# A mixture-of-experts decoder block on one Trainium2 core: six split operations of the next expert's weights move to later steps of the order

## The chip, the cores and the metric

One core of a Trainium2 chip runs the kernel. Its engines are TensorE (PE in the profile, with its weight loads as PEld), VectorE (DVE), ScalarE (ACT), GpSimd (POOL) and SyncE (SP, which here only issues DMAs). The metric is the device time of one execution in microseconds; the kernel before took 1094.59 us in the median of three runs (1091.77 to 1094.7).

## What is computed

A decoder block over 1024 tokens of width 1024 in float32: a gated mixer (a chunked gMLP beside sliding-window attention), a residual sum, then a mixture of 16 experts and a last RMSNorm. Each token goes to two of the 16 experts. The part that matters here is the experts:

```python
for e in range(N_EXPERTS):
    hid = jax.nn.silu(t @ w_gate[e]) * (t @ w_up[e])
    out = out + combine[:, e:e + 1] * (hid @ w_down[e])
```

`w_gate[e]` and `w_up[e]` are 1024 x 512, `w_down[e]` is 512 x 1024. The kernel computes an expert only on the tokens that chose it.

## The kernel before

The products have float32 accuracy, made of three products of numbers that TensorE takes at full rate: every operand is split into a **high part** (a rounded copy, made by ACT) and a **low part** (operand minus high part, made by DVE), and `mm3` (lines 198 to 201) adds high x high, high x low and low x high in PSUM.

**Stages.** After the mixer and the routing (to about 650 us) the tokens lie sorted by expert in DRAM. The loop at line 1674 runs through 16 stages, `e` = 0 to 15, an expert each; a table sets which expert comes when, by its count of tokens. A stage has a **first tile** (the first 128 tokens, or fewer, always computed, `expert_tile`, line 1352) and, only if the expert has more than 128 tokens, a **last tile**, which is computed before the rest of the first tile (`last_tile`, line 1552): a **half tile** for up to 64 more tokens (`half_tile`, line 1461; its names end in `h`), otherwise a full one (names ending in `l`). In this run stages 2, 4, 6, 8 and 10 have a half tile, stages 12 and 15 a full last tile, and stages 3, 5, 7, 9, 11, 13 and 14 none.

**An expert's weights** come as 12 granules of 128 x 1024 numbers (512 KB): granules 0 to 7 hold gate and up (two DMAs of 256 KB each), 8 to 11 down. During stage `e` the granules of the expert of stage `e + 1` are split: `granules.high(g)` is an ACT copy (line 299), `granules.low(g)` a DVE subtraction (line 305 for granules 0 to 7, line 309 for 8 to 11). There are nine raw buffers, so the load of granule `g + 9` is issued behind the low part of `g` (`load_others`, line 315). All loads are issued by SP, in the order of the granules.

**The order of a stage.** Granules 0, 1 and 2 are split at the start (beside the last tile). The table `AHEAD` (line 51) says behind which step of the first tile each further high part (`h3`) and low part (`l3`) is written, for stages 2 to 14. The steps of `expert_tile` are:

- `("k", 0..3)`: gate and up products of the first four granules, for both halves `f` of the hidden width
- `("f0", 5)`: behind granules 4 and 5 of half 0; granules 6 and 7 follow
- then `hidden(0)`: the silu of half 0 (ACT, line 1368) and **the product of activations**, silu times up (DVE, line 1369)
- `("f1", 5)`: behind granules 4 and 5 of half 1; then `hidden_T(0)`: TensorE transposes the product (line 1375), ACT and DVE split it (lines 176 and 177, tile `hT`)
- granules 6 and 7 of half 1, then `hidden(1)`, then `("f1", 7)`
- `down(0)` (line 1413), `hidden_T(1)`, `("y", 0)`, `down(1)`, `("y", 1)`, `down(2)`, `("y", 2)`, `down(3)`

At `("y", 1)` the next stage's tokens X are transposed and split ahead of the table's entries (`transpose_x`, line 1312, tile `xT`; lines 1325, 176, 177). At `("k", 2)` SP loads the tokens of the next stage's last tile into `xt_last` (`last_rows`, line 1444; lines 1453 to 1458), and only if that stage has one. A half tile begins with the transposes of `xt_last` (line 1472) and their split (tile `xT_last`).

An engine runs its instructions in its own order and waits at the head of it. TensorE's, SP's and GpSimd's are taken as written; the order of ACT and DVE comes from a scheduler that follows the written order.

Of the kernel before, what the change touches and what calls it, by code (L numbers as in the profile page):

```python
# [48 lines left out]
FIRST = 3  # L49

AHEAD = {
    ("k", 1): "h3 l3", ("k", 2): "h4 l4", ("k", 3): "h5 l5", ("f0", 5): "h6 l6",
    ("f1", 5): "h7 l7 h8", ("f1", 7): "l8 h9", ("y", 0): "l9 h10", ("y", 1): "l10 h11", ("y", 2): "l11",
}

AHEAD_0 = {("f1", 7): "h3 l3 h4 l4", ("y", 0): "h5 l5 h6 l6 h7 l7", ("y", 1): "h8 l8 h9 l9 h10 l10 h11 l11"}
# [1879 lines left out]
```

## Time and profile before

| What | Value |
|---|---|
| Median of three runs | 1094.59 us (1091.77, 1094.59, 1094.7) |
| The profiled execution's own time | 1091.46 us |
| Its span, first to last instruction | 1089.7 us |
| Mean granted TensorE clock | 0.98 of full speed |
| PE busy | 1023.1 us, 94% of the span |
| DVE busy | 724.8 us, 67% |
| ACT busy | 608.7 us, 56% |
| DMA, mean over the span | 197 GB/s |

The profiled execution is 3.13 us below the median. All times of rows are counted from the start of its span. In a row of the timeline the first number is the start, the second the duration, and what stands in brackets is how long the engine sat idle ahead of it and what ended that. Rows of one line and tile that follow each other without a gap are merged (x3).

### The profile page before, as it was taken

The numbers are of one execution on the slowest core, as the hardware profiler recorded it, in microseconds if no ns is written. First come the engines' busy times: TensorE is split into PE (matmuls) and PEld (weight loads), VectorE is DVE, ScalarE is ACT, GpSimd is POOL, SyncE is SP. The second block draws the span as 40 slices with busy tenths as digits, with TensorE's granted clock in tenths as the row PEclk, the third lists the DMA queues.
The fourth block names the chain that finished last, engine by engine and source line by source line (L and its number), as shares of the span: only waits on it lengthen the run. The fifth ranks groups of instructions, "written<-read, shape, count | busy, mean of one in ns | idle before, by whom it ended". The sixth has DMA issues, their size and how long they took to land. (4 is left out here: it accounts for less than half of the span.)

```text
span 1089.7 us, 15458 instructions
## 1 busy us (share of the span) xinstructions
PE 1023.1 (94%) x4775; PEld 821.1 (75%) x4775; DVE 724.8 (67%) x1584; ACT 608.7 (56%) x1016; POOL 107.6 (10%) x132
## 2 busy tenths in 40 slices
PE   7999899999999999999999958899999999999893
PEld 6778788788888888887888846677777777777682
DVE  6852577675368555776445788978769686848735
ACT  5543465543356464555335447676858686847743
POOL 4001000000004000000001041111111112010020
PEclk9999999999999999999999989999999999999997
DMA  8432545645137413222646546969898989979854
GB/s 248 122 106 102 173 157 166 188 140 184 44 120 273 140 54 97 83 72 68 203 152 215 196 175 223 330 241 319 281 334 258 313 293 285 306 240 309 252 218 191
DMA packets 125478, 214.47 MB, mean 197 GB/s; under 512 B 11563, under 2 KB 58731, under 8 KB 125360
## 3 DMA queue, kind: packets, MB, share of 16 engines
q1 hardware_dynamic: 112016, 176.58, 48.6%
q0 software_dynamic: 7200, 21.20, 7.0%
q10 hardware_dynamic: 6144, 15.27, 3.8%
q8 instruction: 56, 0.92, 0.3%
q14 instruction: 62, 0.51, 0.1%
HBM read 185.46 MB, written 37.63 MB: 205 GB/s over the span
## 5 line engine op out<-in xcount | busy, mean ns | idle before, releaser
L305 DVE SCALAR_TENSOR_TENSOR w_e<-raw_e,g2T,w_e 128x1024 fp32r<-128x1024 f32 x127 | 156.1, 1280 | 22.9 <-ACT w_e L299 16.6
L299 ACT ACTIVATE w_e<-raw_e,g2T 128x1024 fp32r<-128x1024 f32 x127 | 137.5, 1142 | 15.1 <-DMA raw_e<-in_expert_w_up_dram 4.5
L199 PE MATMUL ps_gu<-w_e,xT 128*128 128x512 f32 x256 | 104.2, 407 | 8.9 <-ACT w_e L299 4.1
L201 PE MATMUL ps_gu<-w_e,xT 128*128 128x512 f32 x256 | 101.8, 398 | 1.1 <-DVE xT L177 1.1
L1413 PE MATMUL ps_y<-w_e,hT 128*128 128x512 f32 x384 | 100.4, 404 | 1.1 <-DVE hT L177 0.9
L200 PE MATMUL ps_gu<-w_e,xT 128*128 128x512 f32 x256 | 101.5, 396 | 0.0
L1413 PEld LDWEIGHTS ps_y<-w_e,hT 128*128 128x128 f32 x384 | 69.9, 190 | 17.3 <-DVE hT L177 1.8
L309 DVE TENSOR_TENSOR w_e<-raw_e,w_e 128x1024 fp32r<-128x1024 f32 x63 | 75.0, 1218 | 0.8 <-ACT w_e L299 0.8
L299 ACT ACTIVATE w_e<-raw_e 128x1024 fp32r<-128x1024 f32 x63 | 65.7, 1054 | 0.4 <-DMA raw_e<-in_expert_w_down_dram 0.2
L199 PEld LDWEIGHTS ps_gu<-w_e,xT 128*128 128x128 f32 x256 | 48.7, 190 | 20.7 <-issue 9.7
L201 PEld LDWEIGHTS ps_gu<-w_e,xT 128*128 128x128 f32 x256 | 48.8, 190 | 12.9 <-DVE xT L177 1.5
L200 PEld LDWEIGHTS ps_gu<-w_e,xT 128*128 128x128 f32 x256 | 48.8, 191 | 10.1
L201 PE MATMUL ps_o<-w_wo,ms 128*128 128x512 f32 x128 | 51.3, 402 | 0.0
L200 PE MATMUL ps_o<-w_wo,ms 128*128 128x512 f32 x128 | 51.1, 400 | 0.0
L199 PE MATMUL ps_o<-w_wo,ms 128*128 128x512 f32 x128 | 51.1, 399 | 0.0
L199 PE MATMUL ps_ga<-xh,w_ga 128*128 128x512 f32 x128 | 50.8, 397 | 0.0
L200 PE MATMUL ps_ga<-xh,w_ga 128*128 128x512 f32 x128 | 50.7, 396 | 0.0
L201 PE MATMUL ps_ga<-xh,w_ga 128*128 128x512 f32 x128 | 50.6, 396 | 0.0
L200 PE MATMUL ps_gb<-xh,w_gb 128*128 128x512 f32 x128 | 50.6, 395 | 0.0
L201 PE MATMUL ps_gb<-xh,w_gb 128*128 128x512 f32 x128 | 50.6, 395 | 0.0
L199 PE MATMUL ps_gb<-xh,w_gb 128*128 128x512 f32 x128 | 50.6, 395 | 0.0
L567 PE MATMUL ps_gv<-w_gv,xh 128*128 128x512 f32 x192 | 46.9, 397 | 3.9 <-ACT xh L176 2.5
(540 smaller groups left out, 2379.8 us busy)
## 6 DMA issues: line engine op xcount, KB each, us to landing
raw_e<-in_expert_w_gate_dram SPq DMA_DIRECT2D x127, 256.0 KB
raw_e<-in_expert_w_up_dram SPq DMA_DIRECT2D x127, 256.0 KB
raw_e<-in_expert_w_down_dram SPq DMA_DIRECT2D x63, 512.0 KB
xs_d<-zero ACTq DMA_DIRECT2D x16, 516.0 KB
xt_last<-xs_d SPq DMA_DIRECT2D x32, 258.0 KB
raw_ga<-in_w_in_dram SPq DMA_DIRECT2D x16, 512.0 KB
raw_gb<-in_w_in_dram SPq DMA_DIRECT2D x16, 512.0 KB
raw_wo<-in_w_out_dram SPq DMA_DIRECT2D x16, 512.0 KB
```

The lines of the kernel that those rows point to most:

```text
L199: nc.tensor.matmul(acc, lhi, rhi, start=start, stop=False)
L200: nc.tensor.matmul(acc, lhi, rlo, start=False, stop=False)
L201: return nc.tensor.matmul(acc, llo, rhi, start=False, stop=stop)
L299: nc.scalar.activation(self.split_tiles[g][:, 0, :], self.raw[g], AF.Copy, **scale)
L305: nc.vector.scalar_tensor_tensor(w[:, 1, :], raw, g2T[:, k : k + 1], w[:, 0, :], ALU.mult, ALU.subtract)
L309: nc.vector.tensor_tensor(w[:, 1, :], raw, w[:, 0, :], ALU.subtract)
L567: nc.tensor.matmul(accs[i], xh[a][k // 4][:, k % 4, t], gs[j][:, b, k % 2, :], start=k + a + b == 0, stop=k == KT - 1 and b == 1,)
L1413: nc.tensor.matmul(ys[nh], hT[:, a, k, :], dn[k][:, b, nh * 512 : (nh + 1) * 512], start=k + i == 0, stop=k == FK - 1 and i == 2,)
```

## The change

Only the table `AHEAD` changes: six of the nine low parts that it orders move a step down, high parts stay where they are.

```diff
 AHEAD = {
-    ("k", 1): "h3 l3", ("k", 2): "h4 l4", ("k", 3): "h5 l5", ("f0", 5): "h6 l6",
-    ("f1", 5): "h7 l7 h8", ("f1", 7): "l8 h9", ("y", 0): "l9 h10", ("y", 1): "l10 h11", ("y", 2): "l11",
+    ("k", 1): "h3 l3", ("k", 2): "h4 l4", ("k", 3): "h5 l5", ("f0", 5): "h6", ("f1", 5): "l6 h7 h8",
+    ("f1", 7): "l7 h9", ("y", 0): "l8 h10", ("y", 1): "l9 l10 h11", ("y", 2): "l11",
 }
```

The fourth low part of the first tile, `l6`, goes from `("f0", 5)` behind `hidden(0)`; `l7`, `l8` and `l9` follow a step later each. So `l9`, `l10` and `l11` come behind the split of the next X, where before it was `l10` and `l11`.

Stage 5 (no last tile), DVE, before, from the fourth low part of the first tile to the split of the next X (`w_e` with `g2T` are low parts of granules 0 to 7, without it of 8 to 11; here 5300 is granule 6, 5367 is 7, 5376 is 8, 5525 is 9; the two ISA rows compute the tokens' weights `cw`):

```order
L305 SCALAR_TENSOR_TENSOR w_e_5300<-raw_e_5370,g2T,w_e_5300 128x1024
L1369 TENSOR_TENSOR hid_0_8831<-hid_0_8831,ps_gu_0_8459 128x256
L305 SCALAR_TENSOR_TENSOR w_e_5367<-raw_e_5373,g2T,w_e_5367 128x1024
L177 TENSOR_TENSOR hT_8751<-ps_hT_0_8848,hT_8751 128x256
L1369 TENSOR_TENSOR hid_1_8859<-hid_1_8859,ps_gu_1_8460 128x256
L1399 ISA parts,cw_8862<-meta_8418,own 128x4
L1399 ISA cw_8862 128x1
L309 TENSOR_TENSOR w_e_5376<-raw_e_5379,w_e_5376 128x1024
L177 TENSOR_TENSOR hT_8751<-ps_hT_1_8877,hT_8751 128x256
L309 TENSOR_TENSOR w_e_5525<-raw_e_5382,w_e_5525 128x1024
L177 TENSOR_TENSOR xT_5985<-ps_xT_0_8894,xT_5985 128x512
L177 TENSOR_TENSOR xT_5985<-ps_xT_1_8899,xT_5985 128x512
```

The same place with the change, from the first product of activations to granule 9:

```order
L1369 TENSOR_TENSOR hid_0_8828<-hid_0_8828,ps_gu_0_8459 128x256
L305 SCALAR_TENSOR_TENSOR w_e_5300<-raw_e_5370,g2T,w_e_5300 128x1024
L177 TENSOR_TENSOR hT_8751<-ps_hT_0_8845,hT_8751 128x256
L1369 TENSOR_TENSOR hid_1_8856<-hid_1_8856,ps_gu_1_8460 128x256
L1399 ISA parts,cw_8859<-meta_8415,own 128x4
L1399 ISA cw_8859 128x1
L305 SCALAR_TENSOR_TENSOR w_e_5367<-raw_e_5373,g2T,w_e_5367 128x1024
L177 TENSOR_TENSOR hT_8751<-ps_hT_1_8874,hT_8751 128x256
L309 TENSOR_TENSOR w_e_5376<-raw_e_5379,w_e_5376 128x1024
L177 TENSOR_TENSOR xT_5985<-ps_xT_0_8891,xT_5985 128x512
L177 TENSOR_TENSOR xT_5985<-ps_xT_1_8896,xT_5985 128x512
L309 TENSOR_TENSOR w_e_5525<-raw_e_5382,w_e_5525 128x1024
```

One low part fewer stands ahead of the first product, ahead of both splits of `hT` and ahead of the split of X, and one more behind that. It is so in each of stages 2 to 14.

Stage 5, ACT, with the change, from the high part of granule 6 to the split of the first `hT`; before, the order is the same:

```order
L299 ACTIVATE w_e_5300<-raw_e_5370,g2T 128x1024
L1368 ACTIVATE hid_0_8828<-ps_gu_0_8459 128x256
L299 ACTIVATE w_e_5367<-raw_e_5373,g2T 128x1024
L299 ACTIVATE w_e_5376<-raw_e_5379 128x1024
L176 ACTIVATE hT_8751<-ps_hT_0_8845 128x256
```

Nothing moves here: the split of `hT` stands behind the high parts of granules 7 and 8. The order of ACT, PE, POOL and SP is the same in the whole program.

## Rows read from the trace of the kernel before

**Rows 1.** What TensorE waited for, 690 to 1035 us: us in total, times, longest us.

```profile
PE ps_hT L1375 <- DVE hid L1369: 11.0, 11, 4.0
...
PE ps_xT_8h L1472 <- DMA xt_last<-xs_d: 0.7, 1, 0.7
...
PE ps_xT_12l L1325 <- DMA xt_last<-xs_d: 0.5, 1, 0.5
```

**Rows 2.** Stages 4, 5: PE, PEld, DVE, ACT, POOL busy; clock, DMA share, GB/s.

```profile
751.00:782.00 31.00, 30.65 (x141) 24.16 (x139) 21.90 (x35) 20.31 (x30) 6.10 (x4) 1.00 0.83 279
782.00:801.00 19.00, 17.92 (x85) 14.27 (x83) 16.86 (x21) 15.97 (x21) 2.00 (x2) 1.00 1.03 328
```

**Rows 3.** Timeline of DVE, stage 5 and the start of stage 6.

```profile
783.86 8.47 DVE L305 SCALAR_TENSOR_TENSOR w_e<-raw_e,g2T,w_e 128x1024 fp32r<-128x1024 f32 x7 [0.85 <-issue]
792.24 0.42 DVE L1369 TENSOR_TENSOR hid<-hid,ps_gu 128x256 f32<-128x256 f32 x1
...
798.65 1.29 DVE L177 TENSOR_TENSOR xT<-ps_xT,xT 128x512 fp32r<-128x512 f32 x2 [0.48 <-ACT xT L176]
799.86 2.35 DVE L309 TENSOR_TENSOR w_e<-raw_e,w_e 128x1024 fp32r<-128x1024 f32 x2
802.22 0.29 DVE L177 TENSOR_TENSOR xT_last<-ps_xT_6h,xT_last 128x128 fp32r<-128x128 f32 x1
```

**Rows 4.** Timeline of ACT, stage 5, around the first product of activations.

```profile
790.27 0.38 ACT L1368 ACTIVATE hid<-ps_gu 128x256 f32<-128x256 f32 x1 [0.26 <-PE ps_gu L201]
...
792.07 1.04 ACT L299 ACTIVATE w_e<-raw_e 128x1024 fp32r<-128x1024 f32 x1
```

**Rows 5.** Timeline of PE, stage 5: the transposes and the first product of `down(0)`.

```profile
792.71 0.44 PE L1375 MATMUL ps_hT<-ident,hid 128*128 128x128 f32 x2 [1.08 <-DVE hid L1369]
...
794.38 0.40 PE L1413 MATMUL ps_y<-w_e,hT 128*128 128x512 f32 x1
```

**Rows 6.** Timeline of PE, stage 4 (half tile): the first products of `down(0)`.

```profile
775.17 0.62 PE L1413 MATMUL ps_y<-w_e,hT 128*128 128x512 f32 x2
```

**Rows 7.** Timeline of ACT, stage 4: split of the first `hT`.

```profile
774.54 0.36 ACT L176 ACTIVATE hT<-ps_hT 128x256 fp32r<-128x256 f32 x1
```

**Rows 8.** Timeline of PE: the half tiles of stages 6 and 8.

```profile
801.16 0.71 PE L1472 MATMUL ps_xT_6h<-ident,xt_last 64*128 64x64 f32 x8
...
803.29 1.09 PE L1491 MATMUL ps_gu_6h<-w_e,xT_last 128*128 128x512 f32 x4
...
852.50 0.68 PE L1472 MATMUL ps_xT_8h<-ident,xt_last 64*128 64x64 f32 x8 [0.69 <-DMA xt_last<-xs_d]
```

**Rows 9.** DMA in 40 slices of 0.2 us, 795 to 803 us.

```profile
GB/s 430 379 430 369 420 379 420 411 401 405 419 259 103 228 167 227 195 185 216 206 246 246 277 236 256 297 348 399 348 246 236 328 318 369 379 359 399 348 348 369
```

**Rows 10.** The same, 846 to 854 us.

```profile
GB/s 389 461 451 328 420 369 421 379 431 342 428 267 186 158 217 176 92 145 185 185 258 236 185 174 164 174 236 256 338 318 389 318 266 236 348 348 318 266 420 358
```

**Rows 11.** Timeline of ACT and PE, stage 14.

```profile
1022.11 1.15 ACT L299 ACTIVATE w_e<-raw_e,g2T 128x1024 fp32r<-128x1024 f32 x1 [3.41 <-DMA raw_e<-in_expert_w_up_dram]
1023.17 0.36 ACT L1368 ACTIVATE hid<-ps_gu 128x256 f32<-128x256 f32 x1
...
1024.96 0.44 PE L1375 MATMUL ps_hT<-ident,hid 128*128 128x128 f32 x2 [3.98 <-DVE hid L1369]
```

**Rows 12.** Windows, two waits and what follows: PE busy, clock, DMA share, GB/s.

```profile
678.77:681.55 2.78, 0.01 (x1) 1.00 1.02 355
681.55:685.00 3.45, 3.44 (x15) 1.00 1.03 362
...
1025.30:1028.70 3.40, 3.40 (x10) 0.51 1.06 318
```

**Rows 13.** SP, stage 4: the first load behind the low part of granule 9.

```profile
779.71 0.33 SPq L280 DMA_DIRECT2D raw_e<-in_expert_w_gate_dram  x1
```

**Rows 14.** DMA, 773.5 to 781.6 us: what moved, and what was issued (gate halves).

```profile
DMA packets 1082, 1.98 MB, mean 244 GB/s; under 512 B 116, under 2 KB 116, under 8 KB 1082
...
raw_e<-in_expert_w_gate_dram SPq DMA_DIRECT2D x6, 256.0 KB
```

## The prediction, made blind

> **What bounds the kernel now.** I read the list of waits first, then the windows of two neighbouring stages, then the timelines of DVE, ACT and PE around the moved low parts, and last DMA and SP. TensorE is busy 94% of the span, so only its waits can go. From stage 2 to stage 14 nearly all of its waiting is one wait, the transposes of `hidden_T(0)` for the product of activations: 11.0 us in 11 waits, the longest 4.0 [rows 1]. Ten short ones share the other 7, in stages 2 to 11; stage 5's is 1.08 [rows 5]. The second thing to see is the DMA system. In stage 4, with a half tile, its share is 0.83; in stage 5, without one, 1.03 [rows 2]. So in odd stages the weights stream without a pause, and two rows for DMA `xt_last` (0.7 and 0.5 us, stages 8 and 12) show who is late behind that stream [rows 1].
>
> **Odd stages (3, 5, 7, 9, 11).** In stage 5 DVE runs seven low parts without a break, 8.47/7 = 1.21 us each, and then the product at 792.24 [rows 3]. ACT's silu is ready at 790.27 + 0.38 = 790.65 [rows 4]. Without the seventh low part the product starts at 792.24 - 1.21 = 791.03, after the silu, so the silu is no new wait. PE arrived at 792.71 - 1.08 = 791.63 [rows 5], and the product would end at 791.03 + 0.42 = 791.45. The whole wait of 1.08 goes.
>
> Not all of it arrives. The next in line, `down(0)`, needs ACT's split of `hT`, which the order puts behind the high part of granule 8. That ends at 792.07 + 1.04 = 793.11 [rows 4], the split takes 0.36 [rows 7], so `down(0)` starts at about 793.5 in place of 794.38 [rows 5]: 0.88 gained. The low part itself isn't saved: it runs behind the product, in time that DVE has.
>
> **Even stages (2, 4, 6, 8, 10).** In stage 4 the split of `hT` starts at 774.54 without idle time ahead of it and ends at 774.90 [rows 7], pinned behind the same high part, and `down(0)` starts at 775.17 [rows 6]. Whatever DVE gives, 775.17 - 774.95 = 0.22 is the gain. Together 1.1 per pair of stages, if nothing follows.
>
> **What is late next: the half tile behind an odd stage.** Two gates stand there. The first is DVE. Before, the two low parts between the split of X and `xT_last` end at 799.86 + 2.35 = 802.21 [rows 3]. Now there are three. X's split starts 1.1 earlier, at 797.55, ends at 798.84, and three low parts of 1.18 end at 802.4. The split of `xT_last` is then 0.2 later than before, and can cost a further 0.1 where the third is 1.2 long. Before, it ended at 802.51 and its products began at 803.29 [rows 3, 8], so 0.78 lay between. With PE 1.1 earlier and the split 0.2 to 0.3 later, 0.5 of the 1.1 is eaten, and some 0.55 per pair is left.
>
> The second gate is `xt_last` itself. SP issues it behind weights that fill the queues. In stage 8 PE waits 0.69 for it and starts at 852.50 [rows 8]; DMA's rate had come back over 300 GB/s at 846 + 28 x 0.2 = 851.6 [rows 10], 0.9 earlier. In stage 6 PE shows no wait, starting at 801.16 [rows 8]; the rate comes back at 795 + 26 x 0.2 = 800.2 [rows 9], 0.96 earlier. By that likeness `xt_last` came just in time in stage 6. The stream doesn't depend on the moved low parts but on the loads that earlier ones released, so PE's getting there earlier turns into this wait. I take 0.2 for each of the pairs that end ahead of stages 4, 6 and 10 (the return can be read to within two slices of 0.2 us, so the slack lies between 0 and 0.4, and I take the middle) and 0 for those ahead of 8 and 12, where the wait is there already. Sum: 0.6. The Trainium skill, "DMA: Bandwidth & Descriptors", Specifications, gives about 358 GB/s as the most that HBM feeds a core; slices here show over 400 [rows 9], so no sum of mine goes by it, but the 328 GB/s of stage 5 is close enough that a faster stream isn't to be expected.
>
> **Stages 12 and 13.** They show no wait of this kind worth a row: 0.
>
> **Stage 14.** High part 6 waits 3.41 us for its weights, the silu ends at 1023.17 + 0.36 = 1023.53, and PE starts at 1024.96 after 3.98 us [rows 11]. In between lie low part 6 (1.21 to 1.28) and the product (0.42). Without the low part PE starts at about 1024.03: 0.93 gained, with no half tile behind it. The wait becomes 3.05. Then the clock: after the 3.98 the granted clock was 0.51, the level of 1.2 GHz, and 3.40 us held 10 matmuls; after an earlier wait of 2.78 us it stayed at 1.00 (2.4 GHz), and 3.45 us held 15 [rows 12]. Ten at full rate are 2.3 us, so up to 1.15 more can come back, and at least 0. 3.05 is nearer to 2.78 than to 3.98, so I take the clock as staying; as `hT`'s split is again behind a high part, I count 0.9. The Trainium skill, "TensorE: Matmul & The Clock Gate", HAM oscillation, tells of waits for DMA behind which matmuls start at half rate; the 3.98 agrees with it, the 2.78 shows the other side, and by that rule alone stage 14 would give only 0.93.
>
> **Queues.** The low parts' moves carry the loads behind them. SP issues granule 9's first load at 779.71 in stage 4 [rows 13]; behind X's split (0.48 idle and 1.29 [rows 3]) it comes at about 781.5. From 773.5 to 781.6 six granules of 2 x 256 KB were issued and 1.98 MB moved [rows 14]. Without granule 9's own, 2.62 - 1.98 = 0.64 MB are still queued at 781.6, 1.6 us at 400 GB/s. So I cost it at nothing; the cover is that queue. The loads of 6, 7 and 8 move by one step (about 1 us) with more queued. In odd stages SP is behind in the stream anyway. POOL's queue passes none of the moved rows. The three low parts behind X's split have no reader on PE before the next stage.
>
> **Sum.** 0.6 + 0 + 0.93 + 0.9 = 2.4 us off the profiled execution's 1091.46, or 1089.0. That execution is 3.13 below the median, so on the scale of the runs I predict 1094.59 - 2.4 = **1092.2 us**. About 0.3% (3.3 us) is what a measurement of this kernel can tell from no change; the three runs shown differ by nearly that.
>
> **Rivals.**
> - *The clock falls in stage 14 all the same* (chance 0.22). For it: 3.05 is still a long wait. Then 0.6 + 0.93 = 1.5, 1093.1 us.
> - *The stream of weights isn't a gate* (0.25): `xt_last` comes with PE's pace, because the loads of the stage before, moved too, leave room for it. Then DVE's gate decides: 5 x 0.55 = 2.75, with stage 14's 0.93 to 1.83 3.7 to 4.6; about 1090.4 us. Against it: the two DMA waits that already stand in stages 8 and 12.
> - *Slower: the queue runs empty in even stages* (0.10). If the time from SP's issue to the first packet exceeds the 1.6 us of cover, DMA stands still, granules of the odd stage come that much later, and as that stage has a share of 1.03 nothing catches up: the loss comes out at `xt_last`. At 1 us in each of five pairs, 5 less stage 14's 0.93 is 4.1 more: 1098.7 us. It decides from the point where 0.64 MB is gone before granule 9's load begins. Against it: later granules were queued before too, and DVE reaches low part 11 at the same time.
> - *The change does nothing that the time shows* (0.05): DVE's order does change, but the gain is taken by the two gates and stage 14's DMA; 1094.6 us.
>
> **How the numbers follow.** The forecast has 0.38. Faster by over 0.3% needs 3.3 us: most of the second rival and a share of the forecast's spread, 0.29. Slower by over 0.3%: the third rival and a little spread, 0.09. Within: 0.62. The range reaches from the second rival's end with the runs' spread, 1089.2, to the last one's with the same, 1095.8; left out are most of the slower case and the far tails.
>
> **What would show it.** In the profile after, the wait for the product (11.0 us) should fall to about 3 us, nearly all in stage 14, with 3.05 as its longest. `down(0)` of stage 5 should start 0.88 earlier against the stage's begin, behind ACT. The wait for DMA `xt_last` should grow to stages 4, 6, 8, 10 and 12, some 0.9 each; if instead the half tile's products wait for DVE's `xT_last`, the second rival holds. In stage 14 the clock behind the wait tells forecast from first rival. A share of DMA below 1 in stage 5, or waits of ACT for weights there, would show the third. I am wrong if the even or odd stages' length changes by over 0.6 us a pair.

## The result: slower by 0.6%, and the profile after

The changed kernel took 1101.03 us in the median of 16 runs (1095.94 to 1106.3), the kernel before 1094.64 us in 16 runs beside them (1091.33 to 1097.88). The ratio is 1.0061, with a 95% interval of 1.0046 to 1.0077: **6.4 us slower**, where 2.4 us faster was forecast.

The profiled execution after took 1104.78 us (span 1103.0 us), 3.75 above its median, while that of before lay 3.18 below the median of its 16 runs. So the two profiles differ by more (13.3 us) than the kernels do. Part of that lies ahead of the changed stages: the first `hT` of stage 0 comes 1.86 us later, and stage 1 adds 2.5 us, with a granted clock of 0.50 from 684 to 688 us where before showed 1.00. What follows counts from the half tile of stage 2.

The list of waits of TensorE after the change, 698 to 1056 us (columns as in [rows 1]):

```profile
PE ps_y L1413 <- ACT hT L176: 7.9, 12, 1.9
...
PE ps_xT_12l L1325 <- DMA xt_last<-xs_d: 1.9, 1, 1.9
PE ps_xT_8h L1472 <- DMA xt_last<-xs_d: 1.6, 1, 1.6
PE ps_xT_10h L1472 <- DMA xt_last<-xs_d: 1.1, 1, 1.1
PE ps_xT_4h L1472 <- DMA xt_last<-xs_d: 0.9, 1, 0.9
```

The wait for the product of activations (11.0 us in [rows 1]) is off the head of the list. Two kinds of wait have come in its place: 7.9 us of `down(0)` for ACT's split of `hT`, and four for `xt_last` of 5.5 us together (1.2 in [rows 1]). A wait of 2.15 us for weights at the start of stage 13 only looks new: the same instruction waited 1.63 us before, put down to another releaser (before, then after):

```profile
992.52 0.47 PE L199 MATMUL ps_gu<-w_e,xT 128*128 128x512 f32 x1 [1.63 <-ACT yt L1431]
```

```profile
1005.93 0.47 PE L199 MATMUL ps_gu<-w_e,xT 128*128 128x512 f32 x1 [2.15 <-ACT w_e L299]
```

The windows of stages 4 and 5 (columns as in [rows 2], laid to the same places of the program):

```profile
756.16:787.05 30.89, 30.68 (x140) 24.16 (x139) 20.90 (x34) 19.96 (x29) 5.66 (x4) 1.00 0.85 282
787.05:807.19 20.14, 18.18 (x85) 14.19 (x83) 16.78 (x21) 15.92 (x21) 2.31 (x2) 1.00 0.95 303
```

Stage 4 is 0.1 us shorter and stage 5 is 1.14 longer. In stage 5 the share of DMA fell from 1.03 to 0.95 and the rate from 328 to 303 GB/s [rows 2]: a stream that was full is full no more. What ACT and PE did there:

```profile
799.09 1.06 ACT L299 ACTIVATE w_e<-raw_e 128x1024 fp32r<-128x1024 f32 x1 [1.88 <-DMA raw_e<-in_expert_w_down_dram]
800.06 0.37 ACT L176 ACTIVATE hT<-ps_hT 128x256 fp32r<-128x256 f32 x1
```

```profile
796.75 0.44 PE L1375 MATMUL ps_hT<-ident,hid 128*128 128x128 f32 x2
...
800.48 0.72 PE L1413 MATMUL ps_y<-w_e,hT 128*128 128x512 f32 x2 [1.89 <-ACT hT L176]
```

PE no longer waits for the product: the transposes at 796.75 have no bracket ([rows 5]: 1.08). But ACT's high part of granule 8 now waits 1.88 us for its `w_down`, the split of `hT` stands behind it, and `down(0)` waits 1.89 us for that. The reader sees one wait handed on: DMA, ACT, PE.

**Where the weights became late.** The stretch in which stage 4 hands over to stage 5, on SP, before and after (each with the granule ahead and the load behind low part 9):

```profile
779.12 0.33 SPq L280 DMA_DIRECT2D raw_e<-in_expert_w_up_dram  x1
```

```profile
784.66 0.33 SPq L280 DMA_DIRECT2D raw_e<-in_expert_w_up_dram  x1
787.04 0.33 SPq L280 DMA_DIRECT2D raw_e<-in_expert_w_gate_dram  x1
787.58 1.18 SPq L280 DMA_DIRECT2D raw_e<-in_expert_w_up_dram  x1
789.02 0.33 SPq L280 DMA_DIRECT2D raw_e<-in_expert_w_gate_dram  x1
789.55 0.33 SPq L280 DMA_DIRECT2D raw_e<-in_expert_w_up_dram  x1
790.17 0.33 SPq L280 DMA_DIRECT2D raw_e<-in_expert_w_down_dram  x1
```

Before, the next issue followed after 0.59 us, at 779.71 [rows 13], at SP's own pace. Now it follows after 2.38. The two loads behind it come later as well: those that low parts 10 and 11 release went out at 781.99 and 783.62 before, and go out at 789.02 and 790.17 now. Counted from the split of X (779.45 and 784.50) the three loads are 2.3, 2.0 and 1.5 us later. The cause is in DVE's order, where low part 9 is the first of three:

```profile
784.50 1.29 DVE L177 TENSOR_TENSOR xT<-ps_xT,xT 128x512 fp32r<-128x512 f32 x2 [0.50 <-ACT xT L176]
785.71 3.49 DVE L309 TENSOR_TENSOR w_e<-raw_e,w_e 128x1024 fp32r<-128x1024 f32 x3
```

DMA in 40 slices of 0.2 us and the sum over 8 us, before from 780 and after from 785 us (5 us is the shift of the same place):

```profile
GB/s 399 399 338 287 369 348 338 410 389 461 379 369 369 389 379 400 369 410 379 420 389 451 348 420 389 359 348 369 318 277 338 358 287 328 369 451 338 287 288 412
DMA packets 1429, 2.94 MB, mean 368 GB/s; under 512 B 159, under 2 KB 159, under 8 KB 1426
```

```profile
GB/s 307 318 246 297 277 369 338 389 358 369 399 420 440 399 318 379 266 277 287 307 266 102 154 164 154 225 358 318 338 410 358 215 195 246 236 154 174 143 266 184
DMA packets 1214, 2.28 MB, mean 286 GB/s; under 512 B 135, under 2 KB 135, under 8 KB 1211
```

The rate falls to 102 at 789.2 and comes back over 300 at 785 + 26 x 0.2 = 790.2, 3.2 us after the late issue. These 3.2 us aren't the latency of one load: up to 788.2 the stream still lived on what was queued (351 GB/s from 785 to 788.2). What a load takes from an empty queue stands in the window of [rows 14], before (issue at 774.09, slices of 0.2 us from 773.5):

```profile
GB/s 10 20 20 0 0 0 0 61 81 152 202 324 405 354 405 405 304 152 233 182 192 111 212 324 314 344 334 425 293 364 303 374 354 435 334 293 354 344 354 405
```

The first packets come 0.8 us behind the issue (774.9), a rate over 300 GB/s 1.6 us behind it (775.7).

By 790.2 of the window after the change 0.42 MB less have moved than before (1.57 against 1.99), and by its end 2.94 - 2.28 = 0.66 MB. The last part is not all loss. From 791.2 on GpSimd's own DMA, the outputs `h_d`, runs beside the weights (0.06 MB in this window), and before it began behind the window; over 16 us the gap is 5.56 - 5.07 = 0.49 MB, 1.3 us at 368 GB/s. ACT's 1.88 us come ten microseconds later; that 0.66 MB at 368 GB/s makes 1.8 us is in part the choice of the window.

**The clock.** Between stage 2 and stage 13 the granted clock of before shows no fall from 1.00 (2.4 GHz). After the change it falls to 0.50 (1.2 GHz) for a part of three windows: behind the waits for `xt_last` of stages 8 (1.57 us) and 12 (1.90), and behind the wait of 2.15 us in stage 13 (PE busy, clock, DMA share, GB/s):

```profile
860.00:864.00 4.00, 4.00 (x11) 0.57 1.04 358
...
964.00:968.00 4.00, 2.41 (x11) 0.75 1.02 362
968.00:972.00 4.00, 4.00 (x17) 0.83 0.97 290
...
1008.00:1012.00 4.00, 4.00 (x14) 0.71 0.95 271
```

In the first, PE is busy for all 4 us and runs 11 matmuls of the kind of which [rows 12] holds 15 in 3.45 us at full clock. The half tile of stage 8 began 6.76 us later than before and its `hT` came 8.32 later: 1.56 lost in it, nearly all to the clock. In the last tile of stage 12 it is 1.60 (11.30 to 12.90).

The three falls belong to this one execution. Its mean granted clock is 0.970, with two others the lowest of the 16 runs, whose mean is 0.974; before, the profiled execution has 0.980, while the 95 runs beside the experiments have 0.975. Over 1100 us a clock lower by 0.001 to 0.0015 is 1 to 1.5 us (an estimate, as if TensorE lost half of each microsecond at half rate), so between the medians at most a quarter of the 6.4 us is clock.

How far the profile after lags behind that of before, from the starts of PE's instructions:

| Place | Before, us | After, us | Later by |
|---|---|---|---|
| half tile of stage 2 | 698.69 | 703.04 | 4.35 |
| half tile of stage 4 | 750.51 | 755.67 | 5.16 |
| half tile of stage 6 | 801.16 | 807.35 | 6.19 |
| half tile of stage 8 | 852.50 | 859.26 | 6.76 |
| half tile of stage 10 | 903.12 | 912.74 | 9.62 |
| last tile of stage 12 | 954.29 | 965.59 | 11.30 |
| `down(0)` of stage 13 | 1004.31 | 1019.27 | 14.96 |
| second `hT` of stage 14 | 1029.59 | 1040.94 | 11.35 |
| second `hT` of stage 15's last tile | 1068.16 | 1081.47 | 13.31 |

The lag grows from row to row by 0.6 to 1.7 us (2.9 from stage 8 to 10 and 3.7 behind stage 12's start, with the clock in both). Stage 14 gives 3.6 back, because the 3.98 us wait of [rows 11] doesn't stand there after the change. That the change did this isn't shown (see e5). The 2.0 us of the last row are mostly TensorE's wait for its own sequencer, which comes up again below.

### The profile page after: what moved, and what is told of

Read it like the earlier page. It is cut to its first block, busy times and chain, and to the rows that moved or that the text cites. A ratio compares the mean times of both kernels' runs of the same rounds, so it can differ in the third digit from the quotient of the medians.

```text
span 1103.0 us, 15445 instructions
## 1 busy us (share of the span) xinstructions
PE 1033.4 (94%) x4775; PEld 826.8 (75%) x4775; DVE 724.8 (66%) x1584; ACT 607.7 (55%) x1016; POOL 109.9 (10%) x132
## 5 line engine op out<-in xcount | busy, mean ns | idle before, releaser
L199 PE MATMUL ps_gu<-w_e,xT 128*128 128x512 f32 x256 | 106.5, 416 | 11.3 <-ACT w_e L299 6.2
L201 PE MATMUL ps_gu<-w_e,xT 128*128 128x512 f32 x256 | 103.9, 406 | 1.1 <-DVE xT L177 1.1
L200 PE MATMUL ps_gu<-w_e,xT 128*128 128x512 f32 x256 | 103.9, 406 | 0.0
L299 ACT ACTIVATE w_e<-raw_e 128x1024 fp32r<-128x1024 f32 x63 | 65.8, 1056 | 13.0 <-DMA raw_e<-in_expert_w_down_dram 12.9
L199 PEld LDWEIGHTS ps_gu<-w_e,xT 128*128 128x128 f32 x256 | 50.1, 196 | 23.6 <-issue 12.9
L201 PEld LDWEIGHTS ps_gu<-w_e,xT 128*128 128x128 f32 x256 | 50.2, 196 | 13.4 <-DVE xT L177 1.5
L200 PEld LDWEIGHTS ps_gu<-w_e,xT 128*128 128x128 f32 x256 | 50.1, 196 | 10.5
```

The lines of the kernel that those rows point to most:

```text
L199: nc.tensor.matmul(acc, lhi, rhi, start=start, stop=False)
L200: nc.tensor.matmul(acc, lhi, rlo, start=False, stop=False)
L201: return nc.tensor.matmul(acc, llo, rhi, start=False, stop=stop)
L299: nc.scalar.activation(self.split_tiles[g][:, 0, :], self.raw[g], AF.Copy, **scale)
```

## The experiments

Two theories stood against each other. **Q**: the load behind low part 9 (and those behind it) goes out too late in the even stages, and the odd stages pay. **D**: DVE's own order is the cost, three low parts in a row between the split of X and that of the half tile's X. Ratios are to the kernel before, run on the same chip beside each group (29 to 35 runs), with 12 runs of a kernel (8 of e4, 6 of e11).

**e1: the new order only in the odd stages; e2: only in the even ones.**

```diff
-            for part in (AHEAD_0, AHEAD_1, AHEAD)[min(e, 2)].get(step, "").split():
+            for part in (AHEAD_N if e in (3, 5, 7, 9, 11) else (AHEAD_0, AHEAD_1, AHEAD)[min(e, 2)]).get(step, "").split():
```

(e2 has 2, 4, 6, 8, 10; `AHEAD_N` is the new table.)

> The new order in stages 3, 5, 7, 9 and 11 only, the old one elsewhere. Theory Q (in the even stages, which have a half tile, the loads behind low parts 7 to 11 go out up to 2.3 us later, the stream of weights thins, and the odd stage behind pays at its high part 8 and at xt_last): the odd stages' loads stand in a full queue anyway, so nothing is lost; down(0) of stage 5 comes about 0.9 us earlier and the wait for DMA xt_last takes most of it; 0 to 2 us faster than before. Theory D (three low parts behind the split of X in the odd stages keep the half tile's X split late): all of the loss is here, 5 to 7 us slower than before.

> The new order in stages 2, 4, 6, 8 and 10 only. Theory Q: all of the loss of the change but that of stage 12 is here, 4 to 7 us slower than before; ACT's high part 8 of stage 5 waits 1 to 2 us for its down weights. Theory D: no half tile stands behind an even stage, so no loss; 0 to 1 us faster (0.2 in each of five stages).

e1: 1.0012 (0.999 to 1.0034). e2: 1.0035 (1.0016 to 1.0055). The loss lies in the even stages, as Q said, though 3.8 us is just under its range; D had 5 to 7 us in the odd ones, where e1's interval ends at 3.7. But Q's signs missed twice. In e2 ACT's high part 8 of stage 5 doesn't wait (795.88, no idle time ahead of it), where 1 to 2 us were expected. The three loads of stage 4 go out as late there as after the change (2.53, 4.00 and 5.16 us behind the split of X at 783.23), but the rate doesn't fall under 230 GB/s in the same 8 us, and 2.62 MB move. So late loads don't thin the stream by the same amount at every handover; what grew in e2 is the wait for `xt_last`, 4.2 us in five places for 1.2. And e1 shows no gain. Its waits of PE, 698 to 1056 us:

```profile
PE ps_hT L1379 <- DVE hid L1373: 2.5, 5, 1.0
...
PE ps_xT_12l L1329 <- DMA xt_last<-xs_d: 2.1, 1, 2.1
...
PE ps_xT_10h L1476 <- DMA xt_last<-xs_d: 1.1, 1, 1.1
PE ps_xT_8h L1476 <- DMA xt_last<-xs_d: 1.0, 1, 1.0
PE ps_xT_6h L1476 <- DMA xt_last<-xs_d: 1.0, 1, 1.0
```

(Lines are 4 higher in this kernel.) In the odd stages the product's wait is gone, and about as much stands again at `xt_last` (5.7 us in all for 1.2). The interval, from 1.1 us faster to 3.7 slower, shows neither a gain nor a loss.

**e3: low part 9 back ahead of the split of X; e4: low part 9 alone moved behind it.**

```diff
-    ("f1", 7): "l7 h9", ("y", 0): "l8 h10", ("y", 1): "l9 l10 h11", ("y", 2): "l11",
+    ("f1", 7): "l7 h9", ("y", 0): "l8 l9 h10", ("y", 1): "l10 h11", ("y", 2): "l11",
```

```diff
-    ("f1", 5): "h7 l7 h8", ("f1", 7): "l8 h9", ("y", 0): "l9 h10", ("y", 1): "l10 h11", ("y", 2): "l11",
+    ("f1", 5): "h7 l7 h8", ("f1", 7): "l8 h9", ("y", 0): "h10", ("y", 1): "l9 l10 h11", ("y", 2): "l11",
```

> The change, but the low part of granule 9 stays ahead of the split of X (behind l8 at the step y0). Its load and those of 10 and 11 go out nearly as early as before; only the loads behind 6, 7 and 8 stay a step later. Theory Q with granule 9's load as the main cost: 0 to 2 us slower than before, against 6.5 for the change. If the loads behind 7 and 8 matter as much: 3 to 5 us slower. Theory D: back to within 1 us of before.

> The kernel before, with the low part of granule 9 alone moved behind the split of X; the first products of activations wait as before. Theory Q: the loss comes without any gain at down(0); 3 to 7 us slower than before. Theory D: the split of xT_last is late in the same way, 3 to 7 us slower too, but then the wait is PE's for DVE xT_last and not ACT's for down weights. If the loads behind 6 to 8 were the cost: within 1 us of before.

e3: 1.0015 (0.9998 to 1.0031). e4: 1.0058 (1.0039 to 1.0077). **One of the six moves is the loss**: alone it costs 0.58%, and without it the change is 0.15% off, an interval that holds no change. In e4's profile PE and ACT (second fence) wait, 698 to 1056 us, for:

```profile
PE ps_hT L1375 <- DVE hid L1369: 8.9, 11, 1.3
PE ps_xT_12l L1325 <- DMA xt_last<-xs_d: 2.5, 1, 2.5
...
PE ps_xT_6h L1472 <- DMA xt_last<-xs_d: 1.5, 1, 1.5
```

```profile
ACT w_e L299 <- DMA raw_e<-in_expert_w_down_dram: 8.7, 10, 1.8
```

These are waits for DMA, with none for DVE's `xT_last` beside stage 2's, which was there before. That speaks for Q. ACT's waits alone don't make the price, though: e3's profile has 11.3 us of them (0.2 before) and no loss. What e4 has are waits for `xt_last` of 6.1 us in five places (1.2 before, 3.4 in e3), with nothing gained at the product to set against them, as e1 has. Most of the product's wait is still there in e4: its removal is not what costs.

**e11: DVE's order as before, only the load behind low part 9 issued later** (behind that of low part 10).

```diff
                     granules.low(g)
-                    granules.load_others(g)
+                    if part != "l9" or e < 2:
+                        granules.load_others(g)
+                    if part == "l10" and e > 1:
+                        granules.load_others(g - 1)
```

> The kernel before with the order of DVE untouched; only the load that the low part of granule 9 releases is issued later, behind the load that the low part of granule 10 releases (from stage 2 on). Theory Q (the late load is the whole cost of moving low part 9): as slow as moving it, 4 to 7 us slower than before, with the waits for DMA xt_last of 1 to 2.5 us. If DVE's three low parts in a row behind the split of X are the cost: within 1 us of before.

1.0092 (1.0062 to 1.0121), 6 runs. SP's issues of stage 4:

```profile
785.60 0.33 SPq L280 DMA_DIRECT2D raw_e<-in_expert_w_gate_dram  x1
...
788.76 0.33 SPq L280 DMA_DIRECT2D raw_e<-in_expert_w_down_dram  x1
```

With the one between them, at 787.61, these are 2.54, 4.55 and 5.70 us behind the split of X (783.06); after the change it is 2.54, 4.52 and 5.67. So the loads go out as late as there, while DVE, ACT and TensorE run the order of before. It is as bad or worse, so D isn't needed. It also overshoots Q's 4 to 7 us. Two things stand behind that. The mean granted clock of its runs is 0.970 for 0.975 beside them, some 5 us by the estimate above. And this edit swaps two granules, so that granule 6, which ACT needs first, comes behind granule 7. ACT in stage 5:

```profile
796.74 1.15 ACT L299 ACTIVATE w_e<-raw_e,g2T 128x1024 fp32r<-128x1024 f32 x1 [4.17 <-DMA raw_e<-in_expert_w_up_dram]
797.80 0.36 ACT L1368 ACTIVATE hid<-ps_gu 128x256 f32<-128x256 f32 x1
```

High part 6 waits 4.17 us, and the silu stands behind it. So e11 shows that the place of a load alone can cost this much; it doesn't size the delay by itself.

**e9 and e10: the kernel before and the change, each with half of `w_down` not loaded from expert 3 on** (columns 512 to 1023; old data is used).

```diff
-            return [(lambda r: r, wd[bass.ds(first_row(p) // 2 + (k - KT) * P, P), :])]
+            c = 512 if g >= 36 else 1024
+            return [(lambda r: r[:, 0:c], wd[bass.ds(first_row(p) // 2 + (k - KT) * P, P), 0:c])]
```

> The kernel before with only the first 512 of the 1024 columns of every w_down granule loaded from expert 3 on (the others are left out: old data is used in their place), 17% fewer bytes of weights. A control for the next kernel. Theory Q (the stream of weights is behind the waits): the waits for DMA xt_last and the 3.98 us of stage 14 go; 3 to 6 us faster than before.

> The change with the same half of w_down left out. Theory Q: with a stream that has room the later loads cost nothing and the earlier product is worth what PE waited, so it is 2 to 5 us faster than the same kernel with the order of before. Theory D, or any cost that lies in the order of DVE or ACT itself: still as much slower as the change is, 4 to 7 us.

e9: 0.9939 (0.9917 to 0.9961). e10: 0.9942 (0.9917 to 0.9967); medians 1088.43 and 1087.76 us. e9 itself is 6.7 us faster than before, where 3 to 6 were expected, and its waits for `xt_last` are gone. With room in the stream the change costs nothing: 0.0003 between them in place of 0.0061 (the means of 12 runs each differ by 0.1 us, give or take 1.7). That is Q's test. But it gives nothing either, and there 2 to 5 us were expected. A part is seen at ACT: it waits 5.4 us for weights in e10 and 0.2 in e9, and `down(0)` 3.4 us for ACT, so even this stream brings the weights late for the earlier product. The half tile of stage 6 shows where another part of stage 5's gain stays. TensorE, e9 and e10:

```profile
803.68 0.39 PE L201 MATMUL ps_gu<-w_e,xT 128*128 128x512 f32 x1
803.90 7.03 PE L1492 MATMUL ps_gu_6h<-w_e,xT_last 128*128 128x512 f32 x30
```

```profile
806.86 0.40 PE L201 MATMUL ps_gu<-w_e,xT 128*128 128x512 f32 x1
807.40 7.31 PE L1492 MATMUL ps_gu_6h<-w_e,xT_last 128*128 128x512 f32 x30
```

In e9 the half tile's products follow after 0.22 us and 30 take 7.03; in e10 they follow after 0.54 and take 7.31: 0.3 + 0.3 = 0.6 us of waiting for the split of `xT_last` behind the three low parts. So theory D's mechanism exists. It eats gains; it isn't the loss.

**e5: the new order in stage 14 alone.**

```diff
-            for part in (AHEAD_0, AHEAD_1, AHEAD)[min(e, 2)].get(step, "").split():
+            for part in (AHEAD_N if e == 14 else (AHEAD_0, AHEAD_1, AHEAD)[min(e, 2)]).get(step, "").split():
```

> The new order in stage 14 alone, where hardly any load stands behind the low parts. The sum's own term: 0.9 to 1.8 us faster than before, by whether the clock behind the wait falls; PE's wait for the product there 3.05 us in place of 3.98. If the wait is only carried on (the stream of weights sets the end of the stage): within 0.3 us of before.

0.999 (0.9966 to 1.0015): 1.1 us faster in the ratio, but the interval holds both expectations. Inconclusive. The wait that was to shrink isn't a fixed one either: 3.98 us in the profile of before, 1.08 and 0.99 in those of e7 and e1, which have the same order in stage 14.

**e7: `xt_last` issued two steps earlier, order of before; e8: the same with e3's table.**

```diff
-            if step == ("k", 2):
+            if step == ("k", 0):
                 got["n"] = last_rows(e + 1)
```

> The order of before, with the load of the next last tile's tokens (xt_last and its meta) issued two steps earlier, at the step k0 instead of k2; some 1 to 3 us earlier in SP's queue. If the place of xt_last in the queue is the gate that takes the gain: the waits for DMA xt_last (0.7 and 0.5 us) go, and 0.5 to 2 us faster. If the stream as a whole is the bound: the weights behind it come later by the same time, and it is within 0.5 us of before.

> The change with granule 9's low part back ahead of the split of X, and xt_last issued at the step k0 as well. Theory Q: xt_last's waits are gone, the earlier products of activations are worth what DVE's split of the half tile leaves, so 1 to 3 us faster than before, and as fast as or up to 1 us faster than the early xt_last alone. If the late loads behind 6 to 8 cost as much as the earlier products give: the same as the early xt_last alone, less 0 to 1 us.

e7: 0.998 (0.9956 to 1.0004). e8: 0.9995 (0.9969 to 1.0021). e7's profile has no wait for `xt_last` left, and its 2.2 us lie just over the 0.5 to 2 that were expected, but the interval doesn't exclude no change. e8 isn't better than e7, which the first expectation wanted.

**e12: `xt_last` early, e3's table in stages 3, 5, 7, 9, 11 and 14 only; e13: in those stages also `h8` behind the split of `hT`.**

```diff
-    ("f1", 5): "l6 h7 h8", ("f1", 7): "l7 h9",
+    ("f1", 5): "l6 h7", ("f1", 7): "h8 l7 h9",
```

> xt_last issued at k0; the order with low parts 6, 7 and 8 a step later (9 ahead of the split of X) only in stages 3, 5, 7, 9, 11 and 14, where loads stand in a full queue, the order of before in the others. Theory Q: no later load anywhere that the stream feels; 2 to 4 us faster than before, 1 to 2 faster than the early xt_last alone.

> As the one before, and in those stages ACT's high part of granule 8 behind the split of hT, so that down(0) doesn't stand behind a high part that waits for weights. If that pin took the gain at down(0): 0.5 to 2 us faster than the mix without it. If the stream sets the end of the pair in any case: the same within 0.5 us.

e12: 0.9972 (0.995 to 0.9994), median 1092.26 against 1093.9 us. It is 3.1 us faster than before, within the 2 to 4 us expected, but its interval ends 0.7 us from no change, and it is the best of several kernels tried; so a small gain is likely and not shown beyond doubt. Against e7 alone it can't be told. e13: 0.9989 (0.9965 to 1.0012): the pin behind high part 8 wasn't what held the gain. ACT's waits, 698 to 1056 us, in e12 and then e13:

```profile
ACT w_e L299 <- DMA raw_e<-in_expert_w_down_dram: 8.8, 11, 1.8
```

```profile
ACT w_e L299 <- DMA raw_e<-in_expert_w_down_dram: 4.2, 6, 1.6
```

ACT waits half as long for down weights, and the kernel is no faster for it. e12's 8.8 us are as much as e4's 8.7, without e4's loss.

## Why the prediction was wrong, step by step

- **Odd stages, the product's wait: right.** The 1.08 us at the transposes of stage 5 went, without a new wait at the silu. That `down(0)` is pinned behind high part 8 was right too; that this high part would run at the same time as before was not: it now waits 1.88 us. It was taken as a row's time when it depends on the stream.
- **Even stages: right in kind.** Stage 4's lag fell by 0.2 from its half tile (5.16) to `down(0)` (4.94), as worked out. (The 774.95 in that working stands in no row; with the 774.90 of [rows 7] it is 0.27.)
- **The step that failed is the one on the queues**: "So I cost it at nothing; the cover is that queue." The load was foreseen 1.8 us later (781.5 for 779.71), and it came 1.8 us later against the issue ahead of it. The cover was about right as well: by 787.04 the five granules issued from 779.24 on, 2.62 MB, had moved 2.09 MB, which leaves 0.53, 1.5 us at 351 GB/s. So this load by itself was about covered (an estimate: no run delays one load alone). What failed is that it alone was counted. Against the slower rival the text held that "DVE reaches low part 11 at the same time". But in an even stage X's split comes only 0.2 us earlier, by the text's own reckoning, and DVE then runs three low parts (3.49 us) for two (2.35): low part 11 ends 4.70 us behind the start of X's split and not 3.56. So the loads behind low parts 10 and 11 came 2.0 and 1.5 us late as well, and in the 4.0 us between the end of the issue at 784.66 and 789.02 SP issued 0.52 MB, while the stream at 351 GB/s takes 1.4. In place of nothing, moving low part 9 costs 0.58% (e4: 6.3 us).
- **The slower rival** (0.10) had the consequence: granules late in a stage that has no time to spare, the loss at `xt_last`, and its sign, a share of DMA below 1 in stage 5 (0.95), came. Its condition wasn't what happened. It asked for more than 1.6 us from SP's issue to the first packet, and the row above shows 0.8. The Trainium skill, "DMA: Bandwidth & Descriptors", Specifications, gives about 0.6 us to the first byte on this path; with the 0.35 us that the issue itself takes in the 0.8, the trace about agrees. What isn't settled is the depth of the dip. SP's issue of the second half took 1.18 us in place of 0.33 (787.58), and no run tells why; in e2, with 0.68 at the same place, the loads came as late and the dip stayed shallow.
- **The first gate: right.** In e1, where PE gets there earlier and the even stages' loads are as before, waits of 1.0 us and more for DMA `xt_last` stand in stages 6, 8, 10 and 12. (After the change they stand in 4, 8, 10 and 12, but there the weights are late too.) The 0.2 per pair that I left beside it isn't seen: e1 shows no gain.
- **The second gate: right in size.** 0.5 was said to be eaten at the half tile, 0.6 was measured in e10. The rival that gives 0.55 per pair with a free stream wasn't seen as a gain either (e10 against e9).
- **Stage 14: open.** 0.9 to 1.8 us was said, and 1.83 of the forecast's 2.4 stood on it (0.93 for the wait, 0.9 for the clock); e5 measured 1.1 faster, between 3.7 faster and 1.6 slower. Both terms rest on one execution, with a wait of 3.98 us and a clock of 0.51 behind it. In e7, with the same order there, it is 1.08 us with a clock of 1.00 behind it.
- **The slower rival's price** was 4.1 us on a stall of 1 us in each of five pairs; 6.4 came out. The profile lags 0.6 to 1.7 us more in four of these pairs and 2.9 in one with a fall of the clock. For the clock no term stood: three falls of about 1.6 us in the profile, 1 to 1.5 us between the runs.

Not settled: at the start of stage 15 PE waits 2.2 us for its own sequencer (line 1718) after the change and 0.3 before. The same wait is 1.6 us in e7, which has the order of before, so it isn't the table's doing, but no run here tells what it is.

## What to carry to other kernels

An operation that is off the critical path still hands back a buffer. Before moving it, find the load that its buffer releases **and the loads that come behind it in the same engine's order**, and ask whether what is queued covers the delay of all of them. Where one stage keeps DMA full and its neighbour doesn't, the transfers that start at the handover belong to the full stage. Delaying them cost time there (e2, e4), and removing a wait of TensorE in the full stage moved it to the next thing that the stream brings (e1).

## What the runs showed of the hardware

- The clock fell behind waits as short as 1.57 us (0.57 in the 4 us that follow, stage 8), while a wait of 2.78 us in the profile of before wasn't followed by a fall [rows 12] and one of 2.82 at the same place after was (0.50 from 684 to 688 us). I had argued from the length of the wait. At the start of stage 13 a wait of 1.63 us before wasn't followed by a fall and one of 2.15 after was (0.71 from 1008 to 1012 us). These rows show that the length alone doesn't tell. The Trainium skill, "TensorE: Matmul & The Clock Gate", HAM oscillation, has matmuls start at half rate behind a wait for DMA; stage 8's row agrees.
- SP issues a granule's two DMAs in about 1.1 us (0.54 to 0.59 apart in the bursts), so it feeds some 470 GB/s of gate and up weights, where the stream carried 408 GB/s at its best (797.0 to 801.5 us after the change) and 303 to 328 over stage 5. The three loads issued 2.3, 2.0 and 1.5 us late weren't caught up within 16 us: 0.49 MB were still missing.
- The 328 GB/s of stage 5 isn't a limit of the stream, as the prediction took it: the 408 GB/s are 4.5 us of the same stage.
